# Row steps of 128 in place of even pieces in the final output of a two-layer decoder step

## The chip, the cores and the metric

The kernel runs on one core of one Trainium2 chip. The metric is the device time of one execution in microseconds (us); lower is better. A profiled execution gives, beside its own time, a span from its first to its last recorded event, and all times of instructions below are counted from the start of that span.

## The reference, cut to what matters

One inference step of a decoder of two layers (model width 1024) is computed for 1024 prompt rows with 16 meta rows ahead of them, and for 64 sample rows: an mLSTM layer and a forgetting-attention layer, each followed by a SwiGLU FFN (inner width 2816). The last line is a normalization of each row with a gain:

```python
def rmsnorm(x, g):
    xf = x.astype(jnp.float32)
    r = lax.rsqrt(jnp.mean(xf * xf, axis=-1, keepdims=True) + EPS)
    return (xf * r * g.astype(jnp.float32)).astype(x.dtype)
...
    y = rmsnorm(h, prm['norm_final'])
```

Here h is what stands after the second FFN. The outputs y_prompt (1024 rows of 1024 float32) and y_sample (64 rows) are these normalized rows; the other outputs (states, keys, values) are written far earlier.

## The kernel before, in words

**Layout.** All 1104 rows (64 sample, 16 meta, 1024 prompt) are held transposed: the 1024 features lie over 128 partitions in 8 blocks, the rows along the free axis. The rows are cut into three slices, `TS`: slice 0 has rows 0 to 256, slice 1 rows 256 to 680, slice 2 rows 680 to 1104 (`SL` = 424). `H[t]` is the residual h of slice t, a tile of 128 x 8 x n; the profile calls all three `Ht`. Float32 products are made of three matmuls of a high and a low part; the casts at L253 (ScalarE) and the subtractions at L254 (VectorE) make these parts.

**The last stage.** `ffn` (L1258) ends with the product with w_down. Its steps are listed in `seq`: 22 steps for slice 0, then 7 rounds of 6 groups for slices 1 and 2, each group with up to 24 matmuls (L1629, PSUM tiles `dps`). The weights of a step are loaded ahead by `w_load` (L1466, issue at L1471) from w_down or from the scratch `sD` on SP's queue, five steps before they are used, into one of three places (two `slot` tiles and `fs`); `w_split` cuts them two steps before. The activations come from the scratch `hB` by `h_load` (L1444, issue at L1449) on POOL's queue. At the end of a round the PSUM sums are added to `H` by VectorE (L1290), and `add_sq` (L308) adds up the squares for the norm (L315, L318, L320). The order of the instructions on TensorE, VectorE and ScalarE in this stage is the order in which they are written (`manual_schedule`).

**The final output.** `final` (L1670) is a generator, one for each slice. For slice 0 it is started when slice 0's sums are complete, for slice 1 after the fifth of the seven rounds, and for slice 2 after everything else. For slices 0 and 1 its steps are taken one or two at a time between the groups of matmuls (L1648 and below), so its work stands between theirs on every engine. For each slice:

- `tiles` lists the row ranges. Slice 0 begins with rows 0 to 80 (64 sample rows and 16 meta rows, of which only the 64 are stored), then two pieces of 88; slices 1 and 2 have four pieces of 106. They come from `pieces_of` (L36), which cuts n into m even pieces.
- `root` sums the squares of each tile over the partitions with one small matmul (L1696), takes the square root on ScalarE (L1698), and one reciprocal on VectorE serves the whole slice (L1700).
- `turn` transposes a tile back to rows with eight matmuls against the identity (L1690), four for each half of the features, into PSUM tiles `fin`: a pool of two for slices 0 and 1, of six for slice 2.
- VectorE multiplies each half by root and gain (L1713), 512 features wide, into a buffer `out`.
- SP stores the buffer: y_sample at L1716, y_prompt at L1718. A store has as many rows as its tile, each of 2048 B, and the rows lie 4096 B apart in the output.

The buffers `out` are parts of another slice's `H` that is not in use then: H[2] for slice 0 (6 buffers for 6 pieces), H[0] for slice 1 (4 buffers for 8 pieces), H[1] for slice 2 (6 buffers for 8 pieces). So in slice 1 the fifth piece on VectorE waits for the first store, and in slice 2 the seventh. After slice 0's output H[2] is loaded again from the scratch `hD`, two blocks of features at a time, on POOL's queue (L1645), and each of these loads waits for the stores that still read its part of H[2].

SP issues the stores and the weight loads in one order, in one queue (q1 in the profile).

Of the kernel before, what the change touches and what calls it, by code (L numbers as in the profile page):

```python
# [16 lines left out]
P = 128  # L17
# [6 lines left out]
T0 = NS + NM  # L24
# [11 lines left out]
def pieces_of(n, m=3):  # L36

    w = -(-n // m)
    return [(a, min(a + w, n)) for a in range(0, n, w)]
# [503 lines left out]
def _add(cls):  # L543
    def deco(f):
        setattr(cls, f.__name__, f)
        return f

    return deco
# [1120 lines left out]
@_add(Net)  # L1669
def final(self, H, t, gr, sp, pools):  # L1670

    nc, O = self.nc, self.O
    pp, pn = pools
    s0, s1 = TS[t]
    r = sp.tile([P, 4], F32, name=self.uid("fr"), tag="fr", bufs=2)
    nc.vector.memset(r, 1.0)
    a = 0 if t else T0
    tiles = [(0, T0)] * (t == 0) + [(s0 + a + b, s0 + a + c) for b, c in pieces_of(s1 - s0 - a, 4 if t else 2)]

    out = H[(2, 0, 1)[t]].rearrange("p k n -> p (k n)")  # L1680
    m = out.shape[1] // 512
    out = [out[:, x % m * 512 : x % m * 512 + 512] for x in range(2 * len(tiles))]

    def turn(t0, t1):
        ps = []
        for g in range(2):
            ps.append(pp.tile([P, 512], F32, name=self.uid("fin"), tag="d", bufs=6) if t == 2 else
                      pn.tile([P, 512], F32, name=self.uid("fin"), tag="n"))
            for k in range(4):
                nc.tensor.transpose(ps[g][: t1 - t0, k * P : k * P + P], H[t][:, 4 * g + k, t0 - s0 : t1 - s0], self.ident)  # L1690
        return ps

    def root():
        ss = pn.tile([P, 512], F32, name=self.uid("fss"), tag="n")
        for y, (a, b) in enumerate(tiles):
            nc.tensor.matmul(ss[: b - a, y : y + 1], self.sums[t][:, a - s0 : b - s0], self.ones[:, 0:1],  # L1696
                             start=True, stop=True)
            nc.scalar.activation(r[: b - a, y : y + 1], ss[: b - a, y : y + 1], AF.Sqrt, scale=1.0 / D,  # L1698
                                 bias=self.eps[: b - a])
        nc.vector.reciprocal(r, r)  # L1700

    if t < 2:
        root()
        yield
    for x, (t0, t1) in enumerate(tiles):
        L = t1 - t0
        ps = turn(t0, t1)
        if t == 2 and x == 0:
            root()
        for g in range(2):  # L1710
            gs = slice(g * 512, g * 512 + 512)
            o = out.pop(0)
            nc.vector.scalar_tensor_tensor(out=o[:L], in0=ps[g][:L], scalar=r[:L, x : x + 1], in1=gr[:L, gs],  # L1713
                                           op0=ALU.mult, op1=ALU.mult)
            if t0 == 0:
                nc.sync.dma_start(O["y_sample"].rearrange("b t d -> (b t) d")[:, gs], o[:NS])  # L1716
            else:
                nc.sync.dma_start(O["y_prompt"][0, t0 - T0 : t1 - T0, gs], o[:L])  # L1718
        yield
# [884 lines left out]
```

## Time and profile before

| | |
|---|---|
| median of 3 runs | 2986.3 us (2984.22, 2986.3, 2991.44) |
| the profiled execution | 2990.01 us |
| its span | 2988.3 us |
| mean granted TensorE clock | 0.98 |
| slice 0's output: its pairs of scaled pieces (L1713) begin | 2764.3, 2769.8 and 2773.8 |
| slice 1's output: first and last scaled piece begin | 2893.4 and 2917.2 |
| slice 2's output: first and last scaled piece begin | 2949.6 and 2961.6 |
| stores of y_prompt: issued from, last issue | 2770.5, 2970.3 |
| DMA over the whole span | 156 GB/s on average |

How to read the lines of the profile: the engines are PE (TensorE matmul), PEld (its weight load), DVE (VectorE), ACT (ScalarE), POOL (GpSimd) and SP. A row of the timeline gives start, duration, engine, line of the kernel, operation, output<-input, shapes and count, and in brackets how long the engine stood idle before it and what released it. SPq is SP's queue of issues: the duration there is that of the issuing, not of the transfer. A row of the windows gives a stretch, its length, the busy time and number of instructions of each engine, the granted clock (1.00 is full), the mean busy share of the core's 16 DMA engines and the GB/s moved. A row of the waits gives who waited for whom: us in total, times, longest.

### The profile page before, as it was taken

How to read it: one execution, taken by the hardware profiler on the slowest of the kernel's cores; microseconds unless marked ns; L12 is line 12 of the kernel's file. 1: busy time of each engine (PE TensorE's matmuls, PEld its weight loads, DVE VectorE, ACT ScalarE, POOL GpSimd, SP SyncE). 2: the span in 40 equal slices, each digit the busy share in tenths (PEclk: the TensorE clock that was granted, in tenths of full speed). 3: DMA queues.
4: the chain of work that ended last, by engine and by line, in shares of the span. 5: the costliest groups of instructions: out<-in, count | busy, mean ns of one | idle time of the engine just before them, and what ended most of it. 6: DMA issues, size and time to landing. Idle time of an engine off the chain costs nothing. (4 is left out here: it accounts for less than half of the span.)

```text
span 2988.3 us, 53415 instructions
## 1 busy us (share of the span) xinstructions
PE 2832.9 (95%) x20729; PEld 2669.0 (89%) x20729; DVE 1708.4 (57%) x3296; ACT 1154.8 (39%) x2105; POOL 821.0 (27%) x1209
## 2 busy tenths in 40 slices
PE   7999989999999999999998998998999999999994
PEld 7998879899999999999998886776989999999984
DVE  4132554867777566653555434775486777655752
ACT  5222552422222254343444445776232222224440
POOL 2021332323223221233543003553232232321220
PEclk9999999999999999999999998999999999999996
DMA  6353545344544386644445755443234454446751
GB/s 190 99 138 99 145 121 172 112 138 142 157 156 153 119 274 213 225 160 135 153 137 158 277 215 181 132 159 114 88 117 135 148 163 143 136 162 223 246 173 45
DMA packets 381444, 467.14 MB, mean 156 GB/s; under 512 B 37390, under 2 KB 302566, under 8 KB 380166
## 3 DMA queue, kind: packets, MB, share of 16 engines
q1 hardware_dynamic: 340878, 325.03, 34.2%
q0 software_dynamic: 37904, 137.23, 14.1%
q8 instruction: 163, 2.67, 0.4%
q10 hardware_dynamic: 2408, 1.46, 0.2%
q14 instruction: 91, 0.75, 0.1%
HBM read 325.98 MB, written 137.64 MB: 155 GB/s over the span
## 5 line engine op out<-in xcount | busy, mean ns | idle before, releaser
L1309 PE MATMUL m<-xh,slot 128*128 128x424 f32 x1376 | 399.1, 355 | 0.0
L254 DVE TENSOR_TENSOR slot<-slot,slot 128x1024 fp32r<-128x1024 f32 (+1 forms) x152 | 194.1, 1278 | 157.3 <-ACT slot L253 157.2
L1309 PEld LDWEIGHTS m<-xh,slot 128*128 128x128 f32 x1376 | 258.7, 188 | 7.3 <-issue 0.2
L253 ACT CAST slot<-slot 128x1024 fp32r<-128x1024 f32 (+1 forms) x152 | 152.8, 1006 | 238.6 <-PE dps L1629 89.7
L1309 PE MATMUL m<-xl,slot 128*128 128x424 f32 x688 | 244.4, 355 | 0.6 <-DVE xl L109 0.6
L180 PE MATMUL tmps<-slot,xh 128*128 128x256 f32 (+2 forms) x864 | 244.7, 283 | 0.0
L181 PE MATMUL tmps<-slot,xh 128*128 128x256 f32 (+2 forms) x864 | 243.4, 282 | 0.0
L182 PE MATMUL tmps<-slot,xl 128*128 128x256 f32 (+2 forms) x864 | 242.9, 281 | 0.0
L182 PE MATMUL fps<-xh,slot 128*128 128x256 f32 x688 | 193.6, 281 | 1.6 <-DVE slot L254 1.6
L181 PE MATMUL fps<-xl,slot 128*128 128x256 f32 x688 | 193.5, 281 | 0.0
L180 PE MATMUL fps<-xh,slot 128*128 128x256 f32 x688 | 193.5, 281 | 0.0
L182 PEld LDWEIGHTS tmps<-slot,xl 128*128 128x128 f32 (+1 forms) x864 | 159.1, 184 | 0.0
L180 PEld LDWEIGHTS tmps<-slot,xh 128*128 128x128 f32 (+1 forms) x864 | 158.5, 183 | 0.2 <-issue 0.2
L181 PEld LDWEIGHTS tmps<-slot,xh 128*128 128x128 f32 (+1 forms) x864 | 158.5, 183 | 0.2 <-issue 0.2
L1309 PEld LDWEIGHTS m<-xl,slot 128*128 128x128 f32 x688 | 129.6, 188 | 4.9 <-DVE xl L109 0.9
L180 PE MATMUL mmA<-xh,whi 128*128 128x424 f32 (+1 forms) x384 | 133.5, 348 | 0.5 <-ACT stg L648 0.5
L182 PEld LDWEIGHTS fps<-xh,slot 128*128 128x128 f32 x688 | 130.0, 189 | 2.0 <-DVE slot L254 2.0
L180 PEld LDWEIGHTS fps<-xh,slot 128*128 128x128 f32 x688 | 129.8, 189 | 0.7 <-ACT slot L253 0.4
L181 PEld LDWEIGHTS fps<-xl,slot 128*128 128x128 f32 x688 | 129.6, 188 | 0.3 <-issue 0.2
L1629 PE MATMUL dps<-xh,slot 128*128 128x256 f32 x704 | 127.6, 284 | 1.5 <-ACT xh L253 1.5
L182 PE MATMUL mmA<-xh,wlo 128*128 128x424 f32 (+1 forms) x384 | 126.4, 329 | 0.0
L181 PE MATMUL mmA<-xl,whi 128*128 128x424 f32 (+1 forms) x384 | 126.4, 329 | 0.0
(695 smaller groups left out, 8144.0 us busy)
## 6 DMA issues: line engine op xcount, KB each, us to landing
slot<-in_w_down SPq DMA_DIRECT2D x48, 512.0 KB
slot<-in_w_gate_up SPq DMA_DIRECT2D x36, 512.0 KB
hr<-hB_T POOLq DMA_DIRECT2D x40, 424.0 KB, 4.9
ws<-in_w_down SPq DMA_DIRECT2D x88, 192.0 KB
sD<-ws SPq DMA_DIRECT2D x88, 192.0 KB
kp<-in_cache_k SPq DMA_DIRECT2D x32, 512.0 KB
vp<-in_cache_v SPq DMA_DIRECT2D x32, 512.0 KB
vA<-in_w_gate_up SPq DMA_DIRECT2D x26, 512.0 KB
```

The lines of the kernel that those rows point to most:

```text
L180: mm(ps, sh, mh, start=first, stop=False)
L181: mm(ps, sh, ml, start=False, stop=False)
L182: mm(ps, sl, mh, start=False, stop=last)
L253: self.nc.scalar.copy(hi, src)
L254: self.nc.vector.tensor_tensor(out=lo, in0=src, in1=hi.bitcast(F32), op=ALU.subtract)
L1309: nc.tensor.matmul(u.ps[b], w[p][:, k], x[q][:, k], start=first and k == i == 0, stop=k == 3 and i == 2, skip_group_check=True)
L1629: nc.tensor.matmul(o, p[:, k, ms], q[:, k], start=fresh and k == x == 0, stop=last and k == nk - 1 and x == 2, skip_group_check=True)
```

## The change

Slice 0 keeps its first tile of 80 rows. All other rows are cut in steps of 128 from the start of the slice, and what is left over comes last: slice 0 has 80, 128 and 48 rows in place of 80, 88 and 88; slices 1 and 2 have 128, 128, 128 and 40 in place of four times 106. The number of tiles, and with it the number of transposes, roots, scaled pieces, buffers and stores, stays as it is.

```diff
@@ -1674,8 +1674,8 @@ def final(self, H, t, gr, sp, pools):
     s0, s1 = TS[t]
     r = sp.tile([P, 4], F32, name=self.uid("fr"), tag="fr", bufs=2)
     nc.vector.memset(r, 1.0)
-    a = 0 if t else T0
-    tiles = [(0, T0)] * (t == 0) + [(s0 + a + b, s0 + a + c) for b, c in pieces_of(s1 - s0 - a, 4 if t else 2)]
+    a = s0 if t else T0
+    tiles = [(0, T0)] * (t == 0) + [(b, min(b + P, s1)) for b in range(a, s1, P)]
```

## The prediction

> **What bounds the kernel now.** I read the page first. TensorE is busy for nearly the whole span, but that is an average over all stages, and the change touches only the last 220 us of it.
>
> ```profile
> span 2988.3 us, 53415 instructions
> PE 2832.9 (95%) x20729; PEld 2669.0 (89%) x20729; DVE 1708.4 (57%) x3296; ACT 1154.8 (39%) x2105; POOL 821.0 (27%) x1209
> ```
>
> Next the chain of waits for the end of the span. Its two long pieces from 2949 on are a store of the output and one VectorE operation released by that store.
>
> ```profile
> 2951.06 10.43 DMA out_y_prompt<-Ht
> ...
> 2961.61 0.75 DVE Ht L1713
> ```
>
> The timeline of VectorE and of SP's queue shows the same stretch: six of the eight scaled pieces of slice 2 come in one run, the seventh and the eighth wait for stores to free their buffers, and issuing the eight stores takes SP 23.7 us.
>
> ```profile
> 2949.62 4.04 DVE L1713 SCALAR_TENSOR_TENSOR Ht<-fin,fr,gfin 106x512 f32<-106x512 f32 x6
> 2957.37 0.75 DVE L1713 SCALAR_TENSOR_TENSOR Ht<-fin,fr,gfin 106x512 f32<-106x512 f32 x1 [3.70 <-DMA out_y_prompt<-Ht]
> 2961.61 0.75 DVE L1713 SCALAR_TENSOR_TENSOR Ht<-fin,fr,gfin 106x512 f32<-106x512 f32 x1 [3.49 <-DMA out_y_prompt<-Ht]
> 2950.40 23.68 SPq L1718 DMA_DIRECT2D out_y_prompt<-Ht  x8
> ```
>
> Then busy time by window (columns: PE, PEld, DVE, ACT, POOL, then the clock, the DMA share and GB/s), and SP's own waits.
>
> ```profile
> 2964.00:2966.00 2.00, 0.00 (x0) 0.00 (x0) 0.00 (x0) 0.00 (x0) 0.00 (x0) 0.50 0.13 51
> 2986.00:2988.30 2.30, 0.00 (x0) 0.00 (x0) 0.00 (x0) 0.00 (x0) 0.00 (x0) 0.50 0.03 12
> ```
>
> ```profile
> SPq L2600 <- DMA out_y_prompt<-Ht: 12.7, 1, 12.7
> ```
>
> From 2962.4 no engine computes anything; the kernel waits for eight stores. The DMA share is 0.13, which is 2 of 16 engines, and 51 GB/s is 25.6 for each of the two. A store of 106 rows of 2048 B is 217,088 B, and at 51 GB/s that is 4.24 us: exactly the distance between the two releases, 2957.37 and 2961.61. So **a 106-row store runs on two DMA engines**, and the eight of slice 2 take 8 x 4.24 = 33.9 us after a start of VectorE that lasts 4 us.
>
> The same stores of slice 1 lie in the middle of the last matmuls. SP's queue there:
>
> ```profile
> 2894.14 0.93 SPq L1718 DMA_DIRECT2D out_y_prompt<-Ht  x2
> ...
> 2899.67 3.90 SPq L1718 DMA_DIRECT2D out_y_prompt<-Ht  x2
> 2903.66 5.10 SPq L1471 DMA_DIRECT2D fs<-sD  x1
> 2908.81 14.30 SPq L1718 DMA_DIRECT2D out_y_prompt<-Ht  x4
> 2923.52 3.94 SPq L1471 DMA_DIRECT2D slot<-sD  x1
> ```
>
> The weight loads of L1471 stand behind the stores, both in issue and on the two engines. What waits for them, engine by engine:
>
> ```profile
> 2936.56 0.62 ACT L253 CAST slot<-slot 128x512 fp32r<-128x512 f32 x1 [16.29 <-DMA slot<-sD]
> ```
>
> ```profile
> 2906.37 0.75 DVE L1713 SCALAR_TENSOR_TENSOR Ht<-fin,fr,gfin 106x512 f32<-106x512 f32 x1 [1.30 <-DMA out_y_prompt<-Ht]
> 2912.92 0.75 DVE L1713 SCALAR_TENSOR_TENSOR Ht<-fin,fr,gfin 106x512 f32<-106x512 f32 x1 [5.80 <-DMA out_y_prompt<-Ht]
> 2917.17 0.75 DVE L1713 SCALAR_TENSOR_TENSOR Ht<-fin,fr,gfin 106x512 f32<-106x512 f32 x1 [3.49 <-DMA out_y_prompt<-Ht]
> ```
>
> ```profile
> 2905.13 0.65 PE L1690 MATMUL fin<-ident,Ht 128*106 128x128 f32 x4 [2.64 <-DVE Ht L1713]
> 2907.18 1.10 PE L1690 MATMUL fin<-ident,Ht 128*106 128x128 f32 x4 [1.40 <-DVE Ht L1713]
> ...
> 2920.06 0.46 PE L1629 MATMUL dps<-T_2l,slot 128*128 128x424 f32 x1 [0.21 <-DVE T_2l L254]
> ...
> 2937.67 0.72 PE L1629 MATMUL dps<-T_4h,slot 128*128 128x424 f32 x1 [3.61 <-ACT T_4h L253]
> ```
>
> TensorE itself stands still there for 2.64, 1.40, 0.21 and 3.61 us.
>
> **The change part by part.** Counts stay as they are: three tiles in slice 0 and four in each other slice, two scaled pieces and two stores a tile, the same bytes. What moves is the rows of a store: 88 and 88 become 128 and 48; four times 106 become 128, 128, 128 and 40.
>
> *How many engines a 128-row store gets.* No store of y has 128 rows now. The nearest rows are a store of another tensor from 128 partitions on the same SP queue, alone on the DMA engines:
>
> ```profile
> 2618.72 0.32 SPq L1327 DMA_DIRECT2D hB_B<-Ht  x1
> ```
>
> ```profile
> 2619.00:2620.00 1.00, 1.00 (x7) 0.97 (x6) 0.97 (x1) 0.00 (x0) 0.00 (x0) 1.00 0.44 171
> 2620.00:2621.00 1.00, 1.00 (x7) 0.96 (x7) 0.84 (x2) 0.00 (x0) 0.00 (x0) 1.00 0.13 46
> ```
>
> The two rows hold 171 + 46 = 217 KB, all of that store and nothing else, at a share of 0.44 of 16 engines over a whole microsecond; two engines cannot exceed 0.125. In all it took (0.44 + 0.13) x 16 = 9.1 engine-us, 23.8 GB/s an engine. That the stores of y, with rows 4 KB apart, are not held to two engines whatever their height is shown by those of 88 rows:
>
> ```profile
> 2774.61 0.95 SPq L1718 DMA_DIRECT2D out_y_prompt<-Ht  x2
> ```
>
> ```profile
> 2778.12 0.73 POOL L1645 DMA_DIRECT2D Ht<-hD  x1 [1.27 <-DMA out_y_prompt<-Ht]
> ```
>
> The reload at 2778.12 needs the third of the four 88-row stores landed. Two engines would need 3 x 180,224 B / 51 GB/s = 10.6 us from the first issue at 2770.5, so 2781 or later; it went at 2778.12. I take 16 engines for 128 rows: 262,144 B / (16 x 23.8 GB/s) = 0.7 us a store, against the 0.66 us at which VectorE delivers pieces ((4.04 - 0.75) / 5).
>
> [...]
>
> *Forty rows.* Unknown; 81,920 B. Between 0.2 us on 16 engines and 3.2 us on one (6.4 for the pair). The 88-row store is the nearest row, and it was on far more than two; I take 0.4 us and keep 6 us as the end of the range.
>
> *Tail.* Let S be the start of the first scaled piece (2949.62 now). The span ends at S + 38.7. After: eight pieces without a wait take 7 x 0.66 + 0.75 = 5.4 us, since the first store must free its buffer only by S + 4. TensorE's transposes keep up: they are done by 2954.0 = S + 4.4 today. Then SP issues the last store and it lands. The first store now lands at 2957.3, 6.9 us after its issue at 2950.40, of which 4.24 are data: 2.7 us are fixed. From the eighth landing (2957.3 + 7 x 4.24 = 2987.0) to the end are 1.3 us. That makes 5.4 + 2.7 + 0.4 + 1.3 = 9.8. But 2.7 holds a slow start of two loaded engines, and the data stop at about 2986.5, 1.8 us ahead of the end; counted by that (5.4, issue 0.5, data 0.4, 1.8) it is 8.1. I take S + 8.9, so the tail **saves 29.8 us** (28 to 30.6).
>
> *Middle.* VectorE's wait at 2906.37 goes, so TensorE's second wait, 1.40, goes. The first one, 2.64, stays: it ends with VectorE's own adds (L1290) and the piece ahead. The 0.21 goes, since VectorE's 5.80 and 3.49 go. The last weight load is issued some 15 us sooner and finds empty rings, so the 3.61 goes. Behind both waits the clock had fallen:
>
> ```profile
> 2904.00:2906.00 2.00, 0.65 (x4) 0.40 (x4) 1.07 (x2) 0.05 (x1) 1.07 (x1) 0.98 0.69 217
> 2906.00:2908.00 2.00, 0.82 (x5) 0.81 (x5) 0.75 (x1) 0.35 (x1) 0.00 (x0) 0.50 0.17 68
> 2908.00:2910.00 2.00, 2.00 (x8) 1.88 (x7) 0.00 (x0) 2.00 (x4) 0.00 (x0) 0.50 0.35 110
> 2912.00:2914.00 2.00, 2.00 (x10) 1.91 (x9) 0.75 (x1) 0.00 (x0) 0.35 (x1) 0.82 0.13 50
> ...
> 2938.00:2940.00 2.00, 1.93 (x5) 1.48 (x5) 0.83 (x2) 0.00 (x0) 0.00 (x0) 0.50 0.00 0
> ```
>
> ```profile
> 2915.24 0.55 PE L1629 MATMUL dps<-T_2h,slot 128*128 128x424 f32 x2
> ...
> 2915.82 0.55 PE L1629 MATMUL dps<-T_2h,slot 128*128 128x424 f32 x2
> ...
> 2938.98 0.91 PE L1629 MATMUL dps<-T_4h,slot 128*128 128x424 f32 x2
> ...
> 2940.04 0.91 PE L1629 MATMUL dps<-T_4h,slot 128*128 128x424 f32 x2
> ```
>
> Three matmuls take 0.58 us at full clock and 1.06 at half, so one costs 0.16 us more. The last twelve run from 2937.67 to 2942.7 with a short wait for the low half in it, 5.05 us; at full clock with operands ready, 12 x 0.193 = 2.3 and 0.1 for the start: 2.6 saved. After the earlier wait the clock was at half from 2906 to 2912.7; 4.8 us of it held matmuls, 13.6 of them, 2.2 us in all. As the wait of 2.64 stays, the clock may fall again: between 0 and 2.2, I take 1.1. Sum: 1.4 + 0.2 + 3.6 + 2.6 + 1.1 = **8.9 us** (7.5 to 10.5).
>
> [...]
>
> *Nothing elsewhere.* In slice 0's output TensorE waits for no store, so faster stores there gain nothing; 128 rows on more rings put at most 0.7 us a store in front of a weight load that is issued two groups ahead (24 matmuls, 4.6 us each).
>
> *Sum.* 29.8 + 8.9 = 38.7. The profiled execution took 2990.0 (span 2988.3), so 2951.3. It lies 3.7 above the median of 2986.3, from which the same gain gives 2947.6. The runs shown spread over 7 us, so I forecast **2948**.
>
> **Rivals.** *Tail only.* The last matmuls find another late operand (an activation load on POOL's queue, or the clock falls there for another reason) and the middle gives nothing: 2990.0 - 29.8 = 2960, or 2956 from the median. For it: VectorE, ScalarE and POOL all had slack there only because TensorE was held. Against: the row at 2936.56 names one load, and it stands behind the stores.
>
> *The stores stay on two engines.* If what limits them is the place of their rows, bytes and rate are unchanged, and so are tail and middle: 2986. The 88-row landing and the 128-row store at 0.44 speak against it.
>
> *Slower: one engine.* Were a 128- or 40-row store of y given one engine, as the 106-row one is given two, the 848 rows of a slice would need 67.9 us in place of 33.9. The tail then grows by 34 us, and the last weight load behind slice 1's stores comes up to 34 us later: 2986 + 68 = 3054. It decides as soon as full stores get fewer than two engines; if the remainder alone did, it would cost 6 us and still be faster. Only the lack of any y store of these heights speaks for it.
>
> **How the numbers follow.** Forecast 0.84; tail only 0.09; two engines 0.04; one engine 0.03. The forecast's own bounds, 35.5 to 41 us of gain on the median and 6 for the remainder, with the spread of the runs, give 2941 to 2957; to take in the tail-only case I set 2940 to 2959. Faster or slower by over 0.3% (9 us, about what a measurement of this kernel can tell from no change): faster 0.93, same 0.04, slower 0.03.
>
> **What would show it.** In the profile after: in the tail a DMA share far above 0.13 for a few microseconds and then the end, no VectorE wait for y stores, and S + 8 to S + 10 at the end; in the middle no ScalarE wait for the last sD load, no 3.6 us of TensorE idle ahead of the last twelve matmuls, and those at full clock; the 2.64 us still there. A share of 0.13 after a 128-row store would prove the main step wrong, a new TensorE wait ahead of the last twelve matmuls the second.

## The result and the profile after

The changed kernel takes 2946.7 us (median of 4 runs, 2945.09 to 2950.87) where the kernel before takes 2986.23 (4 runs, 2984.22 to 2991.44): ratio 0.9867, 95% interval 0.985 to 0.9884. The forecast was 2948, range 2940 to 2959.

The page of the changed kernel; its profiled execution took 2947.09 us:

```profile
span 2945.4 us, 53415 instructions
PE 2826.6 (96%) x20729; PEld 2663.4 (90%) x20729; DVE 1706.7 (58%) x3296; ACT 1154.5 (39%) x2105; POOL 825.5 (28%) x1209
```

The same instructions, nearly the same busy times, 42.9 us less span. VectorE and SP's queue at the end:

```profile
2936.74 5.35 DVE L1713 SCALAR_TENSOR_TENSOR Ht<-fin,fr,gfin 128x512 f32<-128x512 f32 x8
2937.52 4.91 SPq L1718 DMA_DIRECT2D out_y_prompt<-Ht  x8
```

All eight scaled pieces come in one run of 5.35 us with no wait for a store, and SP issues the eight stores in 4.9 us in place of 23.7. The windows there (columns as in the prediction), and SP's last wait:

```profile
2938.00:2939.00 1.00, 1.00 (x7) 1.00 (x6) 1.00 (x3) 0.00 (x0) 0.00 (x0) 0.50 0.62 240
2940.00:2941.00 1.00, 0.61 (x6) 0.30 (x3) 1.00 (x3) 0.00 (x0) 0.00 (x0) 1.00 1.00 381
2942.00:2943.00 1.00, 0.00 (x0) 0.00 (x0) 0.09 (x1) 0.00 (x0) 0.00 (x0) 1.00 0.79 287
2943.00:2944.00 1.00, 0.00 (x0) 0.00 (x0) 0.00 (x0) 0.00 (x0) 0.00 (x0) 0.51 0.22 68
```

```profile
SPq L2600 <- DMA out_y_prompt<-Ht: 1.5, 1, 1.5
```

The DMA share is 1.00 at 381 GB/s where it was 0.13 at 51: sixteen engines at 23.8 GB/s each in place of two at 25.6. SP's wait for the stores at the end is 1.5 us in place of 12.7.

In the middle, SP's issues of slice 1's eight stores are short, and the last weight load goes out at 2904.80, 0.8 us after the last of them:

```profile
2888.74 1.01 SPq L1718 DMA_DIRECT2D out_y_prompt<-Ht  x2
2890.53 0.38 SPq L1471 DMA_DIRECT2D slot<-sD  x1
2895.80 1.51 SPq L1718 DMA_DIRECT2D out_y_prompt<-Ht  x2
2897.59 0.38 SPq L1471 DMA_DIRECT2D fs<-sD  x1
2901.23 2.75 SPq L1718 DMA_DIRECT2D out_y_prompt<-Ht  x4
2904.80 0.35 SPq L1471 DMA_DIRECT2D slot<-sD  x1
```

ScalarE's cast of that load now waits for TensorE and not for the load, where it had stood 16.29 us for the load before:

```profile
2912.64 0.62 ACT L253 CAST slot<-slot 128x512 fp32r<-128x512 f32 x1 [2.21 <-PE dps L1629]
```

Of TensorE's four waits in the middle one is left, the 2.6 us ahead of slice 1's last tile; the last twelve matmuls begin without one and give way to the next transposes at 2929.49; the roots of slice 2 follow at 2933.05:

```profile
2901.26 1.60 PE L1690 MATMUL fin<-ident,Ht 128*40 128x128 f32 x8 [2.62 <-DVE Ht L1713]
...
2927.14 0.35 PE L1629 MATMUL dps<-T_4h,slot 128*128 128x424 f32 x1
...
2929.49 0.60 PE L1690 MATMUL fin<-ident,Ht 128*128 128x128 f32 x3
...
2933.05 0.56 PE L1696 MATMUL fss<-ones,ns 128*128 128x1 f32 x2 [1.95 <-DVE fr L1676]
```

To compare executions I use three marks. F is the first root matmul of slice 1, where slice 1's output begins; S is the first scaled piece of slice 2; E is the end of the span. F is 2890.39 before and 2885.00 after:

```profile
2890.39 0.26 PE L1696 MATMUL fss<-ones,ns 128*106 128x1 f32 x2
```

```profile
2885.00 0.28 PE L1696 MATMUL fss<-ones,ns 128*128 128x1 f32 x2
```

So of the 42.9 us, **30.0 lie in the tail** (S to E: 38.68, then 8.66), **7.5 in the middle** (F to S: 59.23, then 51.74), and 5.4 ahead of F. Ahead of F only slice 0's output differs; over the executions profiled for this study F lies anywhere between 2884.7 and 2893.1, and it is 2885.7 in one with slices 0 and 1 untouched (the eighth experiment). Experiment 7 shows that slice 0's part gains nothing. The 5.4 us therefore lie within the spread between executions, and I count them as no gain.

### The profile page after: what moved, and what is told of

Same layout as the page of the kernel before. It is cut to its first block, busy times and chain, and to the rows that moved or that the text cites. A ratio compares the mean times of both kernels' runs of the same rounds, so it can differ in the third digit from the quotient of the medians.

```text
span 2945.4 us, 53415 instructions
## 1 busy us (share of the span) xinstructions
PE 2826.6 (96%) x20729; PEld 2663.4 (90%) x20729; DVE 1706.7 (58%) x3296; ACT 1154.5 (39%) x2105; POOL 825.5 (28%) x1209
## 5 line engine op out<-in xcount | busy, mean ns | idle before, releaser
L1629 PE MATMUL dps<-T_1h,slot 128*128 128x424 f32 x448 | 127.5, 359 | 0.0
```

Of the source, the lines that this page charges most:

```text
L1629: nc.tensor.matmul(o, p[:, k, ms], q[:, k], start=fresh and k == x == 0, stop=last and k == nk - 1 and x == 2, skip_group_check=True)
```

## Experiments

My theory: the number of DMA engines of a store on SP's queue follows from its number of rows, the tail is the time of the stores, and the middle's stall comes from weight loads behind slow stores. The rule I try is one that fits the two shares measured so far (106 rows 0.13, two engines; 128 rows 1.00, sixteen): the largest number up to 16 that divides the rows. Runs 3, 4 and 5 test it. Rivals: the height or evenness of the tiles counts, or the short last store; VectorE's waits for buffers make the middle's stall. Each group of runs has its own runs of the kernel before (medians 2987 to 2990 us), so ratios are compared. The expected times of runs 1 to 8 count from 2986 us for the kernel before, whose runs beside them have a median of 2989.5; all eight came out above what was expected, by 0.2 to 6.2 us. Where an edit adds lines, L1713 and L1718 have a slightly higher number in its rows.

| run | ratio to before (95%) | F to S | S to E |
|---|---|---|---|
| before | 1 | 59.2 | 38.7 |
| changed kernel | 0.9867 (0.985 to 0.9884) | 51.7 | 8.7 |
| 1 slice 2 only | 0.9898 (0.9883 to 0.9913) | 59.0 | 8.7 |
| 2 slice 1 only | 0.997 (0.9958 to 0.9982) | 49.3 | 38.7 |
| 3 106 rows, stores cut at 96 | 0.9873 (0.9853 to 0.9892) | 49.6 | 10.8 |
| 4 steps of 127 | 1.0234 (1.0214 to 1.0254) | 93.2 | 72.6 |
| 5 108, 108, 104, 104 | 0.9874 (0.9858 to 0.9891) | 50.9 | 11.1 |
| 6 remainder first | 0.9868 (0.9852 to 0.9885) | 48.8 | 8.9 |
| 7 slice 0 only | 1.0008 (0.9998 to 1.0017) | 59.1 | 38.7 |
| 8 slice 2's stores on POOL's queue | 0.9906 (0.9889 to 0.9923) | 58.3 | 11.9 |
| 9 slice 1: early stores fast, late ones slow | 1.0028 (1.0018 to 1.0038) | 66.2 | 38.7 |
| 10 one tile between groups | 0.9861 (0.9844 to 0.9877) | 47.8 | 8.8 |
| 11 changed kernel again | 0.988 (0.9864 to 0.9897) | 50.9 | 8.6 |
| 12 one tile, roots together | 0.9852 (0.9835 to 0.9868) | 43.0 | 8.7 |

**1 and 2: one slice at a time.** Each adds, to the kernel before, the steps of 128 for one slice:

```diff
+    if t == 2:
+        tiles = [(s0 + b, s0 + c) for b, c in [(0, 128), (128, 256), (256, 384), (384, 424)]]
```

(`t == 1` in the second.)

> Only slice 2 gets steps of 128 rows; slices 0 and 1 keep even pieces. If the tail's gain is the store rate alone, the end comes 8.7 us after the first scaled piece of slice 2 (38.7 before) and the middle keeps its 3.6 us wait: 2986 - 30 = 2956 us. If the middle's stalls are covered anyway and all of the gain is the tail: 2947 us.

> Only slice 1 gets steps of 128 rows. If the weight loads behind the stores are what held TensorE in the middle, the last twelve matmuls start without the 3.6 us wait and at full clock, and the time falls by 7.5 us (5 to 10, by the phase of the clock): 2979 us. If something else held it, or the gain is given back at the end: 2986 us. The tail stays at 38.7 us after its first scaled piece.

The first took 2960.5 us where before took 2989.56, the second 2981.62. In the first the tail is the short one, and TensorE's wait of 3.6 us ahead of the last twelve matmuls is still there:

```profile
2938.35 0.46 PE L1629 MATMUL dps<-T_4h,slot 128*128 128x424 f32 x1 [3.62 <-ACT T_4h L253]
...
2950.12 5.36 DVE L1715 SCALAR_TENSOR_TENSOR Ht<-fin,fr,gfin 128x512 f32<-128x512 f32 x8
```

In the second no row of the last groups has a wait, and the tail is that of before, to the tenth. The gains are separate: 30.0 and 9.9 us from the traces. By the medians they are 29.1 and 7.9, together 37.0, where the changed kernel gained 39.5.

**3: same tiles, other stores.** All engines work on 106 rows; only the stores of slices 1 and 2 are cut.

```diff
-                nc.sync.dma_start(O["y_prompt"][0, t0 - T0 : t1 - T0, gs], o[:L])
+                for p, q in ((0, 96), (96, L)) if t else ((0, L),):
+                    nc.sync.dma_start(O["y_prompt"][0, t0 - T0 + p : t0 - T0 + q, gs], o[p:q])
```

> Tiles stay at 106 rows on every engine; only each store of slices 1 and 2 is cut in two, rows 0 to 96 and 96 to 106. If the number of DMA engines follows from the rows of a store (largest number up to 16 that divides them: 16 and 10), the time is that of the changed kernel plus 0 to 3 us for eight more issues on SP in the tail: 2947 to 2950 us. If the height of the tiles in the transposes, roots or scaled pieces is what counts: 2986 us.

The ratio is that of the changed kernel. The scaled pieces still have 106 rows and wait for no store; the share is 0.8 (0.13 with the stores in one piece):

```profile
2940.18 5.36 DVE L1713 SCALAR_TENSOR_TENSOR Ht<-fin,fr,gfin 106x512 f32<-106x512 f32 x8 [0.46 <-PE fin L1690]
```

```profile
2944.00:2945.00 1.00, 0.00 (x0) 0.00 (x0) 1.00 (x3) 0.00 (x0) 0.00 (x0) 1.00 0.80 250
```

So the height of the tiles in transposes, roots and pieces has no visible part in the gain: it is the store.

**4: one row less.** Steps of 127 with 43 last, in slices 1 and 2 (the edit of 1 and 2 under `if t:` with these bounds).

> Slices 1 and 2 in steps of 127 rows, 43 last: one row less than in the changed kernel. If the engines of a store are the largest divisor up to 16 of its rows, all these stores run on one engine: DMA share 0.06, 8 stores in 848 x 2048 B / 25.6 GB/s = 68 us, tail 34 us longer than before and the middle up to 34 more: 3040 to 3054 us. If it is fullness of the 128 partitions that counts: 2947 us.

It took 3060.17 us where before took 2989.56: 70.6 us more, where 54 to 68 were expected. SP needs 58.75 us to issue slice 2's stores, the windows of its tail hold one engine (a share of 0.07 at 26 GB/s; 1/16 is 0.063), and the waits for weights grow with the stores:

```profile
2984.51 58.75 SPq L1720 DMA_DIRECT2D out_y_prompt<-Ht  x8
```

```profile
3000.00:3020.00 20.00, 0.00 (x0) 0.00 (x0) 0.74 (x1) 0.00 (x0) 0.00 (x0) 0.50 0.07 26
```

```profile
2943.90 0.72 PE L1629 MATMUL dps<-T_2l,slot 128*128 128x424 f32 x1 [11.02 <-DVE T_2l L254]
...
2971.76 0.72 PE L1629 MATMUL dps<-T_4h,slot 128*128 128x424 f32 x1 [11.24 <-ACT T_4h L253]
```

F to S grows by 33.9 us and S to E by 33.9, to the tenth the 33.9 us that the eight stores of a slice take on one engine beyond their time on two; the 2.8 us by which the medians differ more than that, these traces do not show. 127 and 43 are prime, as the rule under test asks for one engine. Fullness of the 128 partitions is refuted: with 127 rows S to E is 72.6 us, with 106 it is 38.7.

**5: nearly even pieces.** 108, 108, 104 and 104 rows (bounds 108, 216, 320).

> Nearly even pieces, 108, 108, 104 and 104 rows, in slices 1 and 2. If the engines follow from the divisors (12 and 13 engines), the eight stores of slice 2 need 1.74 MB / (12.5 x 24 GB/s) = 5.8 us in place of 34 and the time is that of the changed kernel plus 0 to 3 us: 2947 to 2950 us, DMA share about 0.8 in the tail. If even pieces as such or a height below 128 are what costs: 2986 us.

The ratio is that of the changed kernel, the share in the tail 0.6 to 0.87. The twelve and thirteen of 16 engines that I expected would be 0.75 and 0.81, and the windows lie on both sides of that; the 272 GB/s of this row are 11.4 engines at 23.8:

```profile
2949.00:2950.00 1.00, 0.00 (x0) 0.00 (x0) 0.56 (x1) 0.00 (x0) 0.00 (x0) 1.00 0.87 272
```

So twelve and thirteen fit but are not counted here; the packets are, in the traces of the kernel before and of the changed one: over the stores of slice 2, most often two are in flight together before and sixteen after. Two rows more or fewer than 106 gain nearly all that steps of 128 do (0.9874 beside 0.9867). The rule fits what was measured at 106, 127 and 128 rows, and roughly at 104 and 108; for other heights these three runs do not show it.

**6: the remainder first.** The changed kernel with bounds 40, 168, 296.

> As the changed kernel, but the 40 rows come first in slices 1 and 2. The DMA engines are full in the tail of the changed kernel, so the order of the same bytes changes 0 to 1.5 us: 2947 to 2948 us. If the short last store is what makes the end short: 3 us or more above the changed kernel, 2950 us or later.

Ratio 0.9868, S to E 8.9 us: where the remainder stands does not matter.

**7: slice 0 alone.** 80, 128 and 48 rows, the rest as before.

> Only slice 0 changes, 128 and 48 rows in place of 88 and 88. No TensorE wait named these stores, so no gain: 2986 us within 3. If the faster stores there feed something later (the reload of H[2], weight loads): 1 us or more less beyond the spread.

Ratio 1.0008 (0.9998 to 1.0017): nothing gained, as expected where no wait of TensorE named these stores.

**8: the other queue.** 106 rows everywhere; slice 2's stores go through POOL.

```diff
-                nc.sync.dma_start(O["y_prompt"][0, t0 - T0 : t1 - T0, gs], o[:L])
+                (nc.gpsimd if t == 2 else nc.sync).dma_start(O["y_prompt"][0, t0 - T0 : t1 - T0, gs], o[:L])
```

> Pieces of 106 rows as before; the eight stores of slice 2 alone are issued on POOL's queue in place of SP's. If a store's rows decide the engines on any queue, two engines, share 0.13, 2986 us. If that holds for SP's queue alone and POOL's spreads 106 rows over all engines, the tail ends 9 to 12 us after its first scaled piece: 2957 to 2960 us.

The tail takes 11.9 us, and a window of it reads

```profile
2950.00:2951.00 1.00, 0.00 (x0) 0.00 (x0) 0.75 (x1) 0.00 (x0) 0.38 (x1) 0.74 0.87 272
```

A share of 0.87 with 106 rows, where SP's queue had 0.13: the limit to two engines belongs to SP's queue and not to the rows alone.

**9: what stalls the middle.** In the profile before, VectorE's waits for buffers and the weight loads behind the stores come together. Here slice 1's first four stores are fast, so that VectorE finds its buffers free, and the last four are slow.

```diff
+                c = (96 if x < 2 else 53) if t == 1 else L
+                for p, q in ((0, c), (c, L)):
+                    if p < q:
+                        nc.sync.dma_start(O["y_prompt"][0, t0 - T0 + p : t0 - T0 + q, gs], o[p:q])
```

> Pieces of 106 rows everywhere. In slice 1 the stores of the first two tiles are cut at row 96 (fast, so that VectorE finds its four buffers free), those of the last two at row 53, so that all 53-row halves share one engine: 4 x 8.5 = 34 us from about 2905 on. Slices 0 and 2 as before. If the 3.6 us wait came from weight loads standing behind stores on SP's queue and rings, it comes back though VectorE waits for no store: 6 to 10 us ahead of the last matmuls, time 2985 to 2992 us. If it came from VectorE's waits for buffers: no wait there, middle 10 us shorter, 2979 us.

VectorE, SP, ScalarE and TensorE in this run:

```profile
2904.53 1.40 DVE L1713 SCALAR_TENSOR_TENSOR Ht<-fin,fr,gfin 106x512 f32<-106x512 f32 x2
2906.47 1.60 DVE L1713 SCALAR_TENSOR_TENSOR Ht<-fin,fr,gfin 106x512 f32<-106x512 f32 x2 [0.53 <-PE fin L1690]
```

```profile
2905.31 24.80 SPq L1721 DMA_DIRECT2D out_y_prompt<-Ht  x8
2930.20 4.26 SPq L1471 DMA_DIRECT2D slot<-sD  x1
```

```profile
2943.36 0.62 ACT L253 CAST slot<-slot 128x512 fp32r<-128x512 f32 x1 [29.28 <-DMA slot<-sD]
```

```profile
2944.47 0.72 PE L1629 MATMUL dps<-T_4h,slot 128*128 128x424 f32 x1 [13.53 <-ACT T_4h L253]
```

The 53-row halves run on one engine: between 2918 and 2926 the windows show a share of 0.06 to 0.07 at 25 to 26 GB/s. VectorE waits for no store of slice 1, and TensorE still stands for 13.5 us until the last weight load has landed and been cast. The time is 2997.59 us, ratio 1.0028: above the 2985 to 2992 that I had written down, since the wait came out at 13.5 and not 6 to 10 us. So late weight loads alone are enough for the wait ahead of the last matmuls, and VectorE's waits are not needed for it. Those had a part of their own in the profile before, TensorE's 1.40 us behind VectorE's wait at 2906.37. Whether the load is held by SP's issue (it goes out at 2930.20, 25 us after the stores began) or by the stores ahead of it in the transfer (it lands 13 us after that) is not separated: both are in these rows.

**10, 11 and 12: what is left.** The remaining 2.6 us on TensorE and the roots. In 10, the changed kernel takes at most one tile of slice 1 between two groups:

```diff
-                for _ in range(2 if t and z > 4 and i % 2 else 0 if t and z == 1 and last else 1):
+                for _ in range(2 if after and t and z > 4 and i % 2 else 0 if t and z == 1 and last else 1):
```

12 has this too, and all root matmuls of a slice first with the square roots behind them, two roots in slices 1 and 2 and three in slice 0; 11 is the changed kernel beside it.

```diff
-            nc.scalar.activation(r[: b - a, y : y + 1], ss[: b - a, y : y + 1], AF.Sqrt, scale=1.0 / D,
-                                 bias=self.eps[: b - a])
+        cuts = [(P, 0, 3), (tiles[3][1] - tiles[3][0], 3, 4)] if t else [(b - a, y, y + 1) for y, (a, b) in enumerate(tiles)]
+        for L, y, z in cuts:
+            nc.scalar.activation(r[:L, y:z], ss[:L, y:z], AF.Sqrt, scale=1.0 / D, bias=self.eps[:L])
```

> The changed kernel, with at most one tile of slice 1's output between two groups of matmuls (before: two after every second group of the last two rounds). If the 2.6 us that TensorE still waits come from two tiles of transposes in a row with two PSUM buffers behind VectorE's adds, they go, and the half clock after them: 2.6 to 5 us less than the changed kernel, 2942 to 2944 us. If VectorE's adds alone hold it, the same wait shows at another place: 2947 us.

> The changed kernel itself, beside the next one on one chip: ratio to before 0.987, 2947 to 2950 us by the chip's level. Its trace gives the stretch from the first root matmul of slice 1 to the first scaled piece of slice 2 a second time: 51.7 us before, 48 to 52 by the phase of the clock.

> The changed kernel with one tile of slice 1 between two groups of matmuls, and in slices 1 and 2 one square root for the three full tiles and one for the remainder, behind all four root matmuls, in place of four in turn. If the four turns of TensorE and ScalarE stand on the path, the chain from the last matmul to the first scaled piece loses about 1.5 us, and with the 2.6 us of the two tiles in a row it is 3 to 6 us less than the changed kernel: 2942 to 2946 us. If something else takes their place: as the changed kernel.

In 10 only 0.5 us of the wait is left and F to S is 47.8 us, but its time (2948.73 where before took 2988.89, above the 2942 to 2944 expected) cannot be told from the changed kernel's. 12 takes 2942.48 us (2938.09 to 2946.18), 11 beside it 2952.79 (2951.23 to 2954.28): no run of 12 is as slow as any of 11. Its roots in the tail:

```profile
2926.01 0.97 PE L1696 MATMUL fss<-ones,ns 128*128 128x1 f32 x8 [1.95 <-DVE fr L1676]
```

```profile
2927.01 0.41 ACT L1700 ACTIVATE fr<-fss,eps 128x3 f32<-128x3 f32 x2 [1.97 <-PE fss L1696]
```

```profile
2927.73 5.35 DVE L1714 SCALAR_TENSOR_TENSOR Ht<-fin,fr,gfin 128x512 f32<-128x512 f32 x8
```

From the first root matmul to the first piece are 1.7 us here; the changed kernel needed 3.7 (2933.05 to 2936.74, the clock at 0.50) and 3.0 in run 11. F to S is 43.0 us, 7.9 below run 11; the other 2.4 of the 10.3 us between the medians these traces do not place. Beside run 11 this version is faster. How much of the 10 us carries over is open: the changed kernel's own ratio came out at 0.9867 in one group and 0.988 in another, and 0.9852 lies within the interval of the first.

## Why the prediction was right, point by point

**Two engines now, sixteen after.** Right: shown by the share of 1.00 at 381 GB/s, and from both sides by 3 (0.8), 4 (0.07) and 5 (0.6 to 0.87). Until the result, sixteen for 128 rows of y was my estimate, from a store of 128 partitions at a share of 0.44 and from the landing of 88 rows.

**Tail.** Forecast S + 8.9, measured S + 8.66; saved 29.8 forecast, 30.0 measured. The sum is right, its makeup less so: I let VectorE's pieces set the pace with one short store behind. In fact the DMA engines are full from about 2938.5 to 2942.5 (a share of 0.98 to 1.02), and 1.74 MB at 381 GB/s are 4.6 us, so the stores and the pieces take about equally long and the stores start 1.5 us later. That is also why the 40 rows, for which I took 0.4 us and kept 6 as the end of the range, show in no time: run 6, without them at the end, has nearly the same tail. In the packets of the trace about ten run together at the height of the two 40-row stores.

**Middle.** Forecast 8.9 (7.5 to 10.5), measured 7.5 in this pair of traces, 8.3 in the second trace of the changed kernel (run 11), and 9.9, 9.6, 8.3 and 10.5 in runs 2, 3, 5 and 6. The waits of 1.40, 0.21 and 3.61 us are gone, and the last twelve matmuls take about 2.4 us (2927.14 to 2929.49) in place of 5.1, each as said. The 2.64 us stay, at 2.62. The term of the clock is the one that varies:

```profile
2888.00:2890.00 2.00, 2.00 (x10) 1.91 (x9) 2.00 (x3) 2.00 (x3) 0.00 (x0) 0.60 0.19 76
2890.00:2892.00 2.00, 2.00 (x7) 1.88 (x7) 1.45 (x2) 1.11 (x2) 0.26 (x1) 0.55 0.63 220
...
2902.00:2904.00 2.00, 2.00 (x8) 1.81 (x9) 1.75 (x3) 0.82 (x2) 1.40 (x2) 0.51 0.80 306
2904.00:2906.00 2.00, 2.00 (x8) 1.88 (x8) 2.00 (x3) 0.00 (x0) 2.00 (x1) 0.63 0.23 76
```

After the 2.62 us the clock falls as before, but for 3.4 us (2902.0 to 2905.5) and not for 6.8 (2905.9 to 2912.7): about 0.9 us gained, where I took 1.1. (The times of the falls and rises are worked out from the clocks 0.60, 0.55, 0.51 and 0.63 of these rows, and for the trace before from 0.98 and 0.82, its rows at 2904 and 2912.) But it also falls at 2888.4, behind the four root matmuls, where it did not in the trace of before. About ten matmuls run at half clock there, 0.16 us more each, so this costs some 1.5 us that the sum had put at nothing: 8.9 less 0.2 and 1.5 is 7.2, near the 7.5.

The 1.1 was an estimate between nothing and the 2.2 of the trace before: no run before the result showed whether the clock falls again after the 2.62 us. The fall behind the roots lasts 3.4 us too (2888.4 to 2891.8). No run shows what makes the clock fall there in one execution and not in another, nor the phase of the clock that the ranges of runs 2 and 11 name; what these two gave is 49.3 us from F to S without the fall and 50.9 with it.

What the runs show is that the change does not make this fall: it is there in 1, 7 and 8 too, where slice 1 has its old rows, and in 5, 10 and 11 (behind the roots two matmuls of 424 columns take 0.91 us in place of 0.55), and not in 2, 3, 4, 6, 9 and 12. They show also when it costs time. With slice 1's slow stores, F to S is 59.0, 59.1 and 58.3 us with the fall (1, 7, 8) and 59.2 without (before). With fast stores it is 50.9 to 51.7 with it (changed kernel, 5, 11) and 48.8 to 49.6 without (2, 3, 6). With slow stores the last twelve matmuls begin 47.3 us after F in the trace of before and in that of run 1 (2937.67 and 2938.35, F at 2890.39 and 2891.09), when the late weight load has been cast, without that fall in the one and with it in the other. So the mechanism of the middle was right, and where in the range one execution falls is luck.

**Slice 0.** Nothing, as said (run 7).

**The level.** The sum on the median gave 2947.6, and I wrote 2948; 2946.7 came. That it came so near is in part luck: the medians differ by 39.5 us, the tail and the middle of the traces account for 37.5, and the other 2 lie within what F moves between executions.

**Rivals.** None came true. The slower one was real as a mechanism: it shows at 127 rows (one engine, 0.07), and its 3054 us stand beside 3060 measured. "Tail only" is what run 1 shows.

## What to carry to other kernels

When a stretch shows a flat DMA share of a small n/16, look at the number of rows of the transfer and not at its bytes. In this kernel stores on SP's queue moved at 51 GB/s and a share of 0.13 with 106 rows (two engines), at 26 GB/s and 0.07 with 127 (one), at 381 GB/s and 1.00 with 128 (sixteen), and at up to 293 GB/s with 104 and 108 (about twelve). Try other row counts, or split only the store, since the compute tiles need not change: 106 rows with stores cut at 96 came to a ratio of 0.9873, steps of 128 to 0.9867. The slow stores here also delayed the weight load issued behind them on the same queue, so the price showed far from the store, as a wait for weights (3.61 us of TensorE before, 13.5 in run 9). Whether the load is held back more in its issue or by the stores ahead of it stayed open (run 9).

## What the runs showed of the hardware that I had not expected

Stores on POOL's queue did not have the limit: in run 8, 106 rows moved at a share of 0.87 there, and before at 0.13 on SP's. Issuing was held back with the transfer: eight stores took SP 4.9 us to issue on sixteen engines, 23.7 us on two, and in run 4 58.75 us on one. And the clock fell in seven of the thirteen traces behind root matmuls of one column in turn with ScalarE (to a mean of 0.60 from 2888 to 2890 in the changed kernel), though TensorE is shown busy for 1.9 of the 3 us from 2885 on; with all four in one run it did not fall there, in the one trace of run 12. The windows of the changed kernel, and two of run 12, whose roots begin at 2884.69:

```profile
2885.00:2886.00 1.00, 0.65 (x5) 0.48 (x3) 0.00 (x0) 0.26 (x1) 0.00 (x0) 1.00 0.00 0
2886.00:2887.00 1.00, 0.39 (x3) 0.30 (x2) 0.00 (x0) 0.48 (x2) 0.00 (x0) 1.00 0.00 0
2887.00:2888.00 1.00, 0.90 (x9) 0.89 (x10) 0.22 (x2) 0.67 (x3) 0.00 (x0) 1.00 0.00 0
2888.00:2889.00 1.00, 1.00 (x7) 0.97 (x6) 1.00 (x2) 1.00 (x2) 0.00 (x0) 0.70 0.00 0
```

```profile
2886.00:2888.00 2.00, 2.00 (x12) 1.93 (x12) 1.18 (x2) 2.00 (x4) 0.00 (x0) 1.00 0.00 0
2888.00:2890.00 2.00, 2.00 (x12) 1.95 (x11) 1.18 (x2) 1.52 (x2) 0.53 (x1) 1.00 0.32 71
```
